# One first load for gains, two x tiles and the first weights, and four gate/up tiles held in single PSUM places

## The chip, the cores and the metric

The kernel runs on one core of one Trainium2 chip. A core has a matrix engine (TensorE, PE in the profile, its weight loads PEld), VectorE (DVE), ScalarE (ACT), GpSimd (POOL) and SyncE (SP, which only starts transfers here). Matmuls write to PSUM; DVE and ACT read it from there; all other data lies in SBUF, and transfers from HBM run on 16 DMA engines. The metric is the device time of one execution in microseconds, as the median of several.

## What is computed

Two layers of a decoder trunk on 256 tokens of width 1024, in float32. A layer is: half a gated feed-forward step, a mixing step (four retention heads and eight latent attention heads side by side), and another half feed-forward step. Cut to what matters for the change:

```python
def rms_norm(x, g):
    y = x * lax.rsqrt(jnp.mean(x * x, axis=-1, keepdims=True) + EPS)
    return y * g

def swiglu_ffn(h, w_gate, w_up, w_down):
    return (jax.nn.silu(h @ w_gate) * (h @ w_up)) @ w_down

for l in range(DEPTH):                     # DEPTH = 2, D_FF = 2816
    x = x + 0.5 * swiglu_ffn(rms_norm(x, ffn1_norm[l]), ffn1_w_gate[l], ffn1_w_up[l], ffn1_w_down[l])
    h = rms_norm(x, mix_norm[l])
    ...                                    # retention and attention, with rotary tables cos/sin of the positions
    x = x + jnp.concatenate([y_ret, y_mla], axis=-1) @ w_o[l]
    x = x + 0.5 * swiglu_ffn(rms_norm(x, ffn2_norm[l]), ffn2_w_gate[l], ffn2_w_up[l], ffn2_w_down[l])
```

## The kernel before

x lies transposed in SBUF, as eight tiles (d or k = 0 to 7) of 128 features by 256 tokens. Each float32 number is split into a high and a low part (`split`, L111 to L118): ACT writes the high part, DVE subtracts it from the original and writes the low part. A product of the two is then three terms: high weight by high x, low weight by high x, high weight by low x. One "block" multiplies one 128 by 128 weight block with one x tile. In the usual form it is two matmuls: the high weights stream both parts of x (512 columns), the low weights only the high part (256 columns). High by low lands in other PSUM columns than the rest and is added on eviction.

Weights come as units of 128 by 1024 numbers (512 KB), in the order of their use. `emit_unit` (L131) issues a unit's load on SP's queue into one of four raw buffers and splits it into one of seven pairs of high and low buffers; `get(i, ahead)` (L154) emits units up to `i + ahead`. Two units make one gate/up tile f (128 of the 2816 hidden features, gate and up): the first unit holds k = 0 to 3, the second k = 4 to 7. Units 0 to 3 come in two pieces each; between their pieces SP issues the gains (`gn`) and x in four loads of two tiles.

The norm is applied late. The matmuls run on x times the gain, and the factor 1/rms of each token is multiplied in when a gate/up tile is evicted. `prep` (L191) splits an x tile, `prep_sq` (L196) squares it and adds it up; for the first norm both run on POOL, for all others the square is on ACT and the sum on DVE. `rstd_of` (L227) adds over the partitions with two small matmuls (`ss`), `rstd_rows` takes the power -1/2 on POOL and puts it on a diagonal (`dg`), `rstd_bc` spreads it over the partitions with one matmul (`rb`) and an ACT copy (`rbc`).

`ffn` (L294) runs 22 gate/up tiles and then the down projection. `gu_mm` does a tile's matmuls; a tile's PSUM place has two banks, `ps2` holds two such places in turn. `gu_sum` (L321) copies one half of the sums by ACT and adds the other half by DVE, `gu_evict` (L331) multiplies with `rbc`, takes silu on ACT, multiplies gate by up and splits the result. For the very first feed-forward step (`first`) the tiles 0 to 2 go block by block (`block`), the squares' sum is taken after six k of tile 1 and the spread after three k of tile 2.

The order of the instructions on each engine is set at compile time by a scheduler that takes the program order as priority and fills gaps with later work; `issue_after` and hand-made dependencies without a semaphore tie it down in places. So the load of the constants (`cst`, masks, decays and rotary frequencies) and of the positions, and the rotary tables that `rope_tables` computes from them on DVE with one sine on ACT, come after the first feed-forward step in the program, but run inside it.

## Time and profile before

| | us |
|---|---|
| median of 3 runs | 932.96 (932.96 to 933.67) |
| profiled execution | 933.92 |
| its span, first to last instruction | 932.1 |
| PE busy in the span | 918.2 (99%) |
| PEld busy | 827.6 (89%) |
| DVE busy | 724.4 (78%) |
| ACT busy | 566.7 (61%) |
| POOL busy | 40.0 (4%) |

The busy share of PE contains waits inside pipelined matmuls, so it is an upper bound. A duration is that of one recorded instruction; back-to-back instructions of an engine overlap a little at their ends. "x8" after an instruction means that eight records are merged into one line. The name behind "<-" in brackets is what released an engine after it had been idle.

### The profile page before, as it was taken

To read this page: it belongs to the slowest core of one execution; us is meant where nothing else is said; L and a number is where in the kernel's file an instruction comes from. 1 tells how busy PE (TensorE), PEld (TensorE's weight loads), DVE (VectorE), ACT (ScalarE), POOL (GpSimd) and SP (SyncE) were. 2 spreads that over 40 slices of the span, in tenths; PEclk is the share of its full clock that TensorE was granted. 3 is DMA by queue.
4 is the path that set the end of the run, shared out by engine and by line. 5 is a ranking of instruction groups with operands and counts; after the bars stand their busy time and mean duration, and the time that the engine had idled before them with its cause. 6 is when DMAs were issued, how large, how long until landed. Compare 5 with 4: busy or idle time off the path is not lost.

```text
span 932.1 us, 14689 instructions
## 1 busy us (share of the span) xinstructions
PE 918.2 (99%) x5518; PEld 827.6 (89%) x5518; DVE 724.4 (78%) x1185; ACT 566.7 (61%) x945; POOL 40.0 (4%) x50
## 2 busy tenths in 40 slices
PE   7999999999999999999999999999999999999998
PEld 5988999998788999999999999999978899999998
DVE  6998886668869888886678888776697798888751
ACT  5665665466966666654556566554868575666540
POOL 6001000011100000000000000000000000000000
PEclk9999999999999999999999999999999999999999
DMA  6866666653534756666656566655545356656660
GB/s 233 279 215 195 212 215 214 184 176 112 178 114 134 233 199 202 203 195 213 202 182 203 193 210 191 217 186 181 174 136 158 105 168 213 209 191 208 204 195 23
DMA packets 49750, 173.79 MB, mean 186 GB/s; under 512 B 5648, under 2 KB 6800, under 8 KB 49680
## 3 DMA queue, kind: packets, MB, share of 16 engines
q1 hardware_dynamic: 49680, 172.87, 57.7%
q8 instruction: 43, 0.70, 0.3%
q14 instruction: 27, 0.22, 0.1%
HBM read 171.80 MB, written 1.05 MB: 185 GB/s over the span
## 4 chain that ended last, share of the span: by engine, by line
PE 85%; DVE 6%; DMA 2%; ACT 2%; POOL 2%; issue 1%; SPq 0%; POOLq 0%; ACTq 0%
PE gu L267 28%; PE dn L267 16%; PE gu L272 14%; PE dn L272 8%; PE wo L267 2%; DVE wlo L115 2%; DMA raw<-w 2%; ACT whi L114 1%; PE wo L272 1%; PE rk L473 1%; PE rv L474 1%; POOL acc L206 1%; PE rq L473 1%; PE qtr L642 1%; PE rk L474 1%
## 5 line engine op out<-in xcount | busy, mean ns | idle before, releaser
L115 DVE TENSOR_TENSOR wlo<-raw,whi 128x1024 fp32r<-128x1024 f32 (+2 forms) x316 | 375.6, 1211 | 63.0 <-ACT whi L114 62.7
L114 ACT ACTIVATE whi<-raw 128x1024 fp32r<-128x1024 f32 (+2 forms) x316 | 326.4, 1041 | 142.3 <-PE dn L267 86.8
L267 PE MATMUL gu<-xhl,whi 128*128 128x512 f32 x1360 | 311.3, 380 | 0.5 <-DVE gt L328 0.2
L267 PEld LDWEIGHTS gu<-xhl,whi 128*128 128x128 f32 x1360 | 249.9, 189 | 34.1 <-DVE gt L328 2.9
L272 PEld LDWEIGHTS gu<-xhl,wlo 128*128 128x128 f32 x1360 | 165.7, 192 | 4.8
L272 PE MATMUL gu<-xhl,wlo 128*128 128x256 f32 x1360 | 166.7, 275 | 0.0
L267 PE MATMUL dn<-h,whi 128*128 128x512 f32 x682 | 159.5, 379 | 0.0
L267 PEld LDWEIGHTS dn<-h,whi 128*128 128x128 f32 x682 | 123.7, 190 | 14.5
L114 ACT ACTIVATE h<-gh 128x256 fp32r<-128x256 f32 x88 | 36.6, 416 | 132.5 <-DVE gh L339 132.5
L272 PEld LDWEIGHTS dn<-h,wlo 128*128 128x128 f32 x682 | 87.0, 191 | 3.8
L272 PE MATMUL dn<-h,wlo 128*128 128x256 f32 x682 | 87.4, 275 | 0.0
L328 DVE TENSOR_TENSOR gt<-gu,ga 128x512 f32<-128x512 f32 x88 | 60.8, 690 | 20.6 <-ACT ga L326 19.8
L326 ACT ACTIVATE ga<-gu 128x512 f32<-128x512 f32 x88 | 52.2, 593 | 22.9 <-PE gu L256 7.9
L115 DVE TENSOR_TENSOR h<-gh,h 128x256 fp32r<-128x256 f32 x88 | 37.4, 425 | 35.7 <-ACT h L114 35.7
L335 DVE TENSOR_TENSOR gt<-gt,rbc 128x512 f32<-128x512 f32 x88 | 60.8, 691 | 2.9
L337 ACT ACTIVATE gs<-gt 128x256 f32<-128x256 f32 x88 | 35.6, 405 | 5.4 <-DVE gt L335 5.3
L339 DVE TENSOR_TENSOR gh<-gs,gt 128x256 f32<-128x256 f32 x88 | 36.9, 419 | 0.3 <-ACT gs L337 0.3
L291 DVE SCALAR_TENSOR_TENSOR x<-dn,x 128x256 f32<-128x256 f32 x31 | 12.7, 421 | 29.6 <-PE dn L267 29.6
L118 DVE SCALAR_TENSOR_TENSOR xhl<-x,gn,xhl 128x256 fp32r<-128x256 f32 x48 | 25.0, 532 | 1.0 <-ACT xhl L117 0.8
L117 ACT ACTIVATE whi<-raw,gn 128x256 fp32r<-128x256 f32 (+2 forms) x38 | 20.5, 579 | 8.1 <-PE ckq L475 4.5
L118 DVE SCALAR_TENSOR_TENSOR wlo<-raw,gn,whi 128x256 fp32r<-128x256 f32 (+2 forms) x38 | 20.8, 577 | 5.5 <-ACT whi L117 5.4
L117 ACT ACTIVATE xhl<-x,gn 128x256 fp32r<-128x256 f32 x48 | 23.4, 496 | 1.6 <-DMA x<-xT 1.0
(234 smaller groups left out, 936.5 us busy)
## 6 DMA issues: line engine op xcount, KB each, us to landing
raw<-w SPq DMA_DIRECT2D x310, 512.0 KB, 4.1
raw<-w SPq DMA_DIRECT2D x8, 416.0 KB, 3.3
raw<-w SPq DMA_DIRECT2D x8, 256.0 KB, 5.7
raw<-w SPq DMA_DIRECT2D x4, 384.0 KB, 3.1
x<-xT SPq DMA_DIRECT2D x4, 256.0 KB, 5.9
out_dram<-x SPq DMA_DIRECT2D x8, 128.0 KB, 2.2
cst<-cst SPq DMA_DIRECT2D x1, 1015.0 KB, 8.1
gn<-gains SPq DMA_DIRECT2D x1, 97.0 KB, 2.8
```

The source lines that it names most:

```text
L114: act(out=h, in_=x, func=AF.Copy)
L115: tt(out=lo, in0=x, in1=h.bitcast(F32), op=ALU.subtract)
L117: act(out=h, in_=x, func=AF.Copy, scale=gain)
L118: stt(out=lo, in0=x, scalar=gain, in1=h.bitcast(F32), op0=ALU.mult, op1=ALU.subtract)
L267: mm(out=ps, lhsT=hi, rhs=both(xhl), start=first, stop=last)
L272: mm(out=ps[:, :S], lhsT=lo, rhs=halves(xhl[:, 0]), start=False, stop=False)
L326: act(out=mem4(a), in_=mix4(ps[:, :, :S]), func=AF.Copy)
L328: tt(out=mem4(t), in0=mix4(ps[:, :, S:]), in1=mem4(a), op=ALU.add)
L335: tt(out=t, in0=t, in1=st.rbc.unsqueeze(1).broadcast_to([P, 2, S]), op=ALU.mult)
L337: act(out=s, in_=t[:, 0], func=AF.Silu)
L339: tt(out=hf, in0=s, in1=t[:, 1], op=ALU.mult)
L473: mm(out=o, lhsT=xh, rhs=wh, start=(k == 0), stop=False)
```

## The change

The gains, the first two x tiles and the first 128 by 256 weights become one DRAM array, loaded by one transfer of 128 rows of 962 numbers (481 KB). The order of the first loads is then: unit 2 (first half of tile f1), the rest of unit 0, x tiles 2 to 5, unit 1, unit 3, x tiles 6 and 7. Their splits follow a list written out by hand, and `program_order` keeps the order of the program on every engine inside its block.

The tiles f0 and f1 are multiplied side by side (`FIRST_ORDER`), then f2 and f3. Each block of these four tiles is three matmuls of 256 columns (`block3`) that add up in one PSUM place of one bank, so that two tiles share what one took. The squares are taken by ACT (`prep_sq_all`, three instructions) and added by DVE (three) after units 4 and 5 have been split. The sum over the partitions comes after seven k of f2, the spread after three k of f3; `gu_scale` evicts such a tile in one DVE instruction with the norm multiplied in, and so the four tiles stay in PSUM until the norm is there. Nothing of the norm is left on POOL but the power and the identity.

The rotary tables and their loads move from behind the first feed-forward step to behind its tile 14; the loads are tied behind the last weight load issued by then.

```diff
+FIRST_ORDER = [(0, 0), (1, 0), (1, 1), (0, 1)] + [(f, k) for k in range(2, KD) for f in range(2)]
...
+    @contextmanager
+    def program_order():
+        cur = nc.cur_bb
+        n = len(cur.bb.instructions)
+        yield
+        assert nc.cur_bb is cur
+        last = {}
+        for i in cur.bb.instructions[n:]:
+            if i.engine in last:
+                tc.add_manual_dep(i, last[i.engine].name,
+                                  mybir.DependencyInfo(mybir.DependencyClass.NoSync, mybir.DependencyReason.DATA),
+                                  reason="program_order")
+            last[i.engine] = i
...
+        skip = 2 * P if i == 0 else 0
+        last_load[0] = nc.sync.dma_start(out=raw[:, skip:n], in_=src[:, skip:])
         segs = gains or [(c, step, None) for c in range(0, n, step)]
-        for c, w, g in segs:
-            split(hi[:, c:c + w], lo[:, c:c + w], raw[:, c:c + w], g)
-        emitted.append((hi, lo))
+        if i == 0:
+            segs = [(0, skip, None), (skip, 2 * P, None), (4 * P, 4 * P, None)]
+        emitted[i] = (hi, lo)
+        return [lambda c=c, w=w, g=g: split(hi[:, c:c + w], lo[:, c:c + w], w00 if c < skip else raw[:, c:c + w], g)
+                for c, w, g in segs]
...
+    def prep_sq_all(st):
+        h = KD * S // 2
+        sq = [hp.tile([P, h], F32, tag=f"h{8 + i}", name=f"sqw{i}") for i in range(2)]
+        act(out=sq[0], in_=xt[:, :h], func=AF.Square)
+        act(out=sq[1][:, :2 * S], in_=x01, func=AF.Square)
+        act(out=sq[1][:, 2 * S:], in_=xt[:, h:], func=AF.Square)
+        tt(out=sq[0], in0=sq[0], in1=sq[1], op=ALU.add)
+        tt(out=sq[0][:, :2 * S], in0=sq[0][:, :2 * S], in1=sq[0][:, 2 * S:], op=ALU.add)
+        st.acc = tp.tile([P, S], F32, tag="acc", name="acc")
+        tt(out=st.acc, in0=sq[0][:, :S], in1=sq[0][:, S:2 * S], op=ALU.add)
...
+    def block3(o, hi, lo, xhl, first, last):
+        mm(out=o, lhsT=hi, rhs=halves(xhl[:, 0]), start=first, stop=False)
+        mm(out=o, lhsT=lo, rhs=halves(xhl[:, 0]), start=False, stop=False)
+        return mm(out=o, lhsT=hi, rhs=halves(xhl[:, 1]), start=False, stop=last)
...
+            if first and f < 4:
+                if f not in pgu:
+                    pgu[f // 2 * 2] = pgu[f // 2 * 2 + 1] = ps2(f"gu{f}")
+                ps = pgu[f][:, f % 2]
+                for k in ks:
+                    hi, lo = get(gu[2 * f + k // 4], 0)
+                    for j in range(2):
+                        c = slice((k % 4 * 2 + j) * P, (k % 4 * 2 + j + 1) * P)
+                        m = block3(ps[:, j * S:(j + 1) * S], hi[:, c], lo[:, c], st.xhl[k], k == 0 and j == 0, k == KD - 1 and j == 1)
+                return m
...
+            if first and f < 4:
+                rb4 = as_ts(st.rbc).unsqueeze(1).broadcast_to([P, 2, 2, P])
+                tt(out=mem4(t), in0=mix4(ps[:, f % 2].rearrange("p (j c) -> p j c", j=2)), in1=rb4, op=ALU.mult)
...
         if first:
-            m = gu_mm(1, range(6))
-            with tc.issue_after(m.ins):
+            with program_order():
+                for f, k in FIRST_ORDER:
+                    gu_mm(f, (k,))
+                get(gu[4], 0)
+                get(gu[5], 0)
+                prep_sq_all(st)
+                get(gu[6], 0)
+                get(gu[7], 0)
+                gu_mm(2, range(7))
                 rstd_of(st)
-            rstd_rows(st)
-            gu_mm(1, range(6, KD))
-            gu_sum(0)
-            m = gu_mm(2, range(3))
-            with tc.issue_after(m.ins):
+                rstd_rows(st)
+                get(gu[8], 0)
+                gu_mm(2, (7,))
+                gu_mm(3, range(3))
                 rstd_bc(st)
+                gu_scale(0)
+                gu_scale(1)
             gu_evict(0)
             gu_evict(1)
-            gu_mm(2, range(3, KD))
+            gu_mm(3, range(3, KD))
             gu_evict(2)
+            gu_evict(3)
...
+            if first and f == 14:
+                first()
...
-    get(0, 1)
-    for d in range(KD):
-        prep(d, st, gn[:, 0, G_F1 + d:G_F1 + d + 1])
-    get(3, 0)
-    for d in range(KD):
-        prep_sq(d, st, True)
+    order[:4] = [2, 0, 1, 3]
+    nc.sync.dma_start(out=head_t, in_=first_d)
+    pcs = {}
+    pcs[2] = load_unit(2)
+    pcs[0] = load_unit(0)
+    nc.sync.dma_start(out=xt[:, :4 * S], in_=xT_d[:, :4 * S])
+    pcs[1] = load_unit(1)
+    pcs[3] = load_unit(3)
+    nc.sync.dma_start(out=xt[:, 4 * S:], in_=xT_d[:, 4 * S:])
+    gp = lambda d: gn[:, 0, G_F1 + d:G_F1 + d + 1]
+    with program_order():
+        for i, d in ((0, 0), (2, 1), (0, None), (0, 2), (2, 3), (1, 4), (3, 5), (1, 6), (3, 7)):
+            pcs[i].pop(0)()
+            if d is not None:
+                prep(d, st, gp(d))
...
-            nc.sync.dma_start(out=cst, in_=cst_d)
-            nc.sync.dma_start(out=posi, in_=pos_d)
-            cs = rope_tables()
+            def tables():
+                with tc.issue_after(last_load[0].ins):
+                    nc.sync.dma_start(out=cst, in_=cst_d)
+                    nc.sync.dma_start(out=posi, in_=pos_d)
+                cs_.append(rope_tables())
+            cs_ = []
+            ffn(st, *e["f1"], n1, col(G_MIX), tables)
```

## Rows read from the trace of the kernel before

**Rows 1.** Busy time by stretch: start:end, length, each engine's busy time (records), clock, DMA.

```profile
core 0: us, PE busy (x) PEld busy (x) DVE busy (x) ACT busy (x) POOL busy (x), PEclk, DMA share, GB/s
6.78:22.36 15.58, 12.00 (x56) 8.53 (x56) 13.72 (x16) 8.84 (x16) 13.85 (x15) 1.00 0.74 265
...
48.00:83.00 35.00, 34.52 (x206) 29.84 (x205) 32.21 (x61) 21.16 (x35) 3.15 (x8) 1.00 0.64 196
83.00:131.00 48.00, 48.00 (x294) 44.03 (x293) 42.72 (x59) 30.46 (x49) 0.00 (x0) 1.00 0.64 214
131.00:932.00 801.00, 794.11 (x4792) 717.93 (x4790) 611.21 (x1016) 486.74 (x817) 20.32 (x17) 1.00 0.56 180
```

**Rows 2.** Timeline, PE's opening: start, duration, engine, line, instruction, count, what it waited for.

```profile
6.78 0.48 PE L252 MATMUL gu<-xhl,whi 128*128 128x512 f32 x1 [1.79 <-DVE xhl L118]
...
15.86 0.38 PE L252 MATMUL gu<-xhl,whi 128*128 128x512 f32 x1
...
20.29 0.38 PE L256 MATMUL gu<-xhl,whi 128*128 128x512 f32 x1
...
22.36 0.61 PE L231 MATMUL ss<-ones,acc 128*128 128x1 f32 x4 [1.69 <-POOL acc L206]
...
22.83 0.36 PE L255 MATMUL gu<-xhl,wlo 128*128 128x256 f32 x1
...
29.89 1.89 PE L267 MATMUL gu<-xhl,whi 128*128 128x512 f32 x8
```

**Rows 3.** Timeline, PE: the low-weight matmuls of tiles f3, f6, f12 and f13.

```profile
31.62 1.95 PE L272 MATMUL gu<-xhl,wlo 128*128 128x256 f32 x16
...
47.34 1.95 PE L272 MATMUL gu<-xhl,wlo 128*128 128x256 f32 x16
...
80.87 1.95 PE L272 MATMUL gu<-xhl,wlo 128*128 128x256 f32 x16
...
86.11 1.95 PE L272 MATMUL gu<-xhl,wlo 128*128 128x256 f32 x16
```

**Rows 4.** Timeline: first load's issue, first ACT splits, each released by a landing.

```profile
0.74 0.39 SPq L141 DMA_DIRECT2D raw<-w  x1
...
3.64 0.63 ACT L114 ACTIVATE whi<-raw 128x512 fp32r<-128x512 f32 x1 [1.41 <-DMA raw<-w]
...
5.28 0.91 ACT L117 ACTIVATE xhl<-x,gn 128x256 fp32r<-128x256 f32 x2 [1.00 <-DMA x<-xT]
...
7.68 0.63 ACT L114 ACTIVATE whi<-raw 128x512 fp32r<-128x512 f32 x1 [1.50 <-DMA raw<-w]
```

**Rows 5.** DMA, 0 to 12 us: rate in 40 slices of 0.3 us.

```profile
GB/s 0 0 0 0 0 41 130 300 292 310 224 325 219 164 212 178 198 198 198 164 123 137 225 321 355 341 335 376 396 382 410 403 403 403 403 396 376 423 382 396
```

**Rows 6.** DVE splits, min/median/max ns: weights to 14 us, x to 18, x later.

```profile
L115 DVE TENSOR_TENSOR wlo<-raw,whi x4: 679/693/1097, 4.3 to 12.4; 128x512 fp32r<-128x512 f32 x4
...
L118 DVE SCALAR_TENSOR_TENSOR xhl<-x,gn,xhl x8: 473/870/945, 5.8 to 14.2; 128x256 fp32r<-128x256 f32 x8
...
L118 DVE SCALAR_TENSOR_TENSOR xhl<-x,gn,xhl x16: 475/480/485, 149.3 to 301.0; 128x256 fp32r<-128x256 f32 x16
```

**Rows 7.** Timeline, PE at the end: first matmul of the first and last of 22 three-matmul blocks.

```profile
921.08 0.27 PE L399 MATMUL dn<-h,whi 128*128 128x256 f32 x1
...
928.11 0.28 PE L399 MATMUL dn<-h,whi 128*128 128x256 f32 x1
```

**Rows 8.** Timeline, the norm's chain: power on POOL, spread row on ACT.

```profile
23.25 0.71 POOL L216 TENSOR_TENSOR rstd<-ms,mhalf 128x2 f32<-128x2 f32 x1 [0.94 <-DVE ms L233]
...
26.82 0.38 ACT L247 ACTIVATE rbc<-rb 128x256 f32<-128x256 f32 x1
```

**Rows 9.** The constants' load (KB, us to landing), and a wait in 48 to 83 us.

```profile
cst<-cst SPq DMA_DIRECT2D x1, 1015.0 KB, 8.1
...
PEld gu L267 <- DVE gt L328: 2.9, 6, 0.6
```

**Rows 10.** Costliest groups of the page: the weight loads of the high parts.

```profile
L267 PEld LDWEIGHTS gu<-xhl,whi 128*128 128x128 f32 x1360 | 249.9, 189 | 34.1 <-DVE gt L328 2.9
```

More of the change, by code (lines that the diff above doesn't have):

```diff
@@ L1 @@
 import math
-from contextlib import ExitStack
+from contextlib import ExitStack, contextmanager
 import numpy as np
@@ L121, in body, with load_unit @@
     units = []
-    emitted = []
+    emitted = {}
+    order = []
     off = [0]
+    last_load = [None]
     def add_unit(ncols, pieces=1, gains=None):
         units.append((off[0], ncols, pieces, gains))
+        order.append(len(units) - 1)
         off[0] += ncols
         return len(units) - 1
-    def emit_unit():
-        o, n, pieces, gains = units[len(emitted)]
-        i = len(emitted)
+    def load_unit(i):
+        o, n, pieces, gains = units[i]
         assert n == WIDTHS[i]
@@ L138, in emit_unit @@
         step = n // pieces
-        dstep = step if i < 4 else n
-        for c in range(0, n, dstep):
-            nc.sync.dma_start(out=raw[:, c:c + dstep], in_=src[:, c:c + dstep])
-            if i == 0 and c == 0:
-                nc.sync.dma_start(out=gn, in_=gn_d)
-            if i < 2:
-                xs = slice(UW * i + c, UW * i + c + dstep)
-                nc.sync.dma_start(out=xt[:, xs], in_=xT_d[:, xs])
-        segs = gains or [(c, step, None) for c in range(0, n, step)]
-        for c, w, g in segs:
-            split(hi[:, c:c + w], lo[:, c:c + w], raw[:, c:c + w], g)
-        emitted.append((hi, lo))
+        skip = 2 * P if i == 0 else 0
+        last_load[0] = nc.sync.dma_start(out=raw[:, skip:n], in_=src[:, skip:])
+        segs = gains or [(c, step, None) for c in range(0, n, step)]
+        if i == 0:
[3 more added lines that the diff above has]
+                for c, w, g in segs]
     def get(i, ahead=2):
         while len(emitted) <= min(i + ahead, len(units) - 1):
-            emit_unit()
+            for piece in load_unit(order[len(emitted)]):
+                piece()
         return emitted[i]
-    xt = xp.tile([P, KD * S], F32, tag="x", name="x")
-    x = [xt[:, d * S:(d + 1) * S] for d in range(KD)]
-    gn = const.tile([P, L, GR], F32, name="gn")
+    head_t = const.tile([P, L * GR + 2 * S + 2 * P], F32, name="first")
+    gn = head_t[:, :L * GR].rearrange("p (l c) -> p l c", l=L)
+    x01 = head_t[:, L * GR:L * GR + 2 * S]
+    w00 = head_t[:, L * GR + 2 * S:]
+    xt = xp.tile([P, (KD - 2) * S], F32, tag="x", name="x")
+    x = [x01[:, d * S:(d + 1) * S] for d in range(2)] + [xt[:, d * S:(d + 1) * S] for d in range(KD - 2)]
     cst = const.tile([P, CW], F32, name="cst")
@@ L194, in prep, with prep_sq @@
         st.xhl.append(xhl)
[L196 removed]
+    def prep_sq(d, st):
         sq = tp.tile([P, S], F32, tag="sq", name="sq", bufs=3)
[L198 to L201 removed]
+        act(out=sq, in_=x[d], func=AF.Square)
         if d == 0:
@@ L247, in rstd_bc @@
         act(out=st.rbc, in_=pb[:, :S], func=AF.Copy)
-    def block(ps, hi, lo, xhl, k, last):
-        if k == 0:
-            mm(out=ps, lhsT=hi, rhs=both(xhl), start=True, stop=False)
-            mm(out=ps[:, :S], lhsT=lo, rhs=halves(xhl[:, 0]), start=False, stop=False)
-        else:
-            mm(out=ps[:, :S], lhsT=lo, rhs=halves(xhl[:, 0]), start=False, stop=False)
-            return mm(out=ps, lhsT=hi, rhs=both(xhl), start=False, stop=last)
+    def block3(o, hi, lo, xhl, first, last):
+        mm(out=o, lhsT=hi, rhs=halves(xhl[:, 0]), start=first, stop=False)
+        mm(out=o, lhsT=lo, rhs=halves(xhl[:, 0]), start=False, stop=False)
+        return mm(out=o, lhsT=hi, rhs=halves(xhl[:, 1]), start=False, stop=last)
     turn = [0]
@@ L301, in gu_mm @@
             ps = pgu[f]
-            if first and f < 3:
-                for k in ks:
-                    hi, lo = get(gu[2 * f + k // 4])
-                    for j in range(2):
-                        c = slice((k % 4 * 2 + j) * P, (k % 4 * 2 + j + 1) * P)
-                        m = block(ps[:, j], hi[:, c], lo[:, c], st.xhl[k], k, k == KD - 1)
-                return m
             for u in range(2):
@@ L367, in ffn @@
             gu_evict(1)
-        for f in range(3 if first else 2, NF):
+        for f in range(4 if first else 2, NF):
             gu_mm(f)
             gu_evict(f)
+            if first and f == 14:
+                first()
         pss = {}
```

48 lines of the change are left out of this document (24 added, 24 removed).

## The prediction

> **What bounds the kernel now.** I read the stages first: busy time by stretch of the span [rows 1]. From 83 us to the end TensorE (PE) has almost no idle time (48.00 of 48.00 us, then 794.11 of 801.00), so what follows the first feed-forward's opening is a rigid tail: what the opening saves moves the end by as much. In 6.78 to 22.36 us PE is busy for only 12.00 of 15.58 us, while VectorE (DVE) has 13.72 and GpSimd (POOL) 13.85. So I read PE in order of time next [rows 2]. Its first real matmul starts at 6.78 us and waited for the low half of x. Tile f0 (16 blocks, one for each of 8 k and of gate and up) lasts until 15.86. After 20.29 it waits for the sum of squares, whose two matmuls start at 22.36; f3 starts at 29.89. Then the los of one tile after the other [rows 3]: 31.62 to 47.34 us are three tiles of 5.24 us, 0.33 per block, with no stall. So f4 starts at 29.89 + 5.24 = 35.13. From 47.34 to 80.87 six tiles take 33.53 us instead of 31.44: 2.1 us are lost there, and tile 86.11 - 80.87 = 5.24 is normal again.
>
> PE's work up to f4 is 64 blocks x 0.33 = 21.1 us and twice 0.47 (22.83 - 22.36, [rows 2]; the broadcast of the norm taken at the same) = 22.0 us. It starts f4 at 35.13, so 13.1 us are lost: 6.78 before the first matmul, 15.86 - 6.78 - 5.3 = 3.8 in f0, the rest (2.5) in f1 and f2, mostly the wait for the squares.
>
> **The change part by part.** *First load.* Before, weights of 256 KB land at 3.64 us, and x lands at 5.28, by when 609 KB (two pieces and 97 KB of gains) have been asked for [rows 4]. One load of 481 KB lies between: 3.64 + 225/353 x 1.64 = 4.7 us. The first weight piece is half of the 0.63 us form, some 0.4 us of ScalarE (ACT), then half of the 0.91 us for two x tiles [rows 4]: the high halves are there at 5.5 us, first matmul 5.6, 1.2 us sooner. The trace shows 2.9 us from the issue of a 256 KB piece at 0.74 us to the split that it released at 3.64 [rows 4]. The Trainium skill, "DMA: Bandwidth & Descriptors", section "Anatomy of one DMA — SWDGE (gpsimd) path", fits about 2.0 us plus bytes over 436 GB/s (for another issuing path), an estimate of 2.6 us for 256 KB and 3.1 for 481 KB; by it the first load is there at 3.9 us and the forecast below would be 925.2 instead of 926.0. The measured piece is already 0.3 us over that fit, so I stay with the rows.
>
> *The loads behind it* are the unknown. In the 0.3 us slices of [rows 5] the transfers run at about 300 GB/s at first, fall to 120 to 220 between 4 and 6.6 us, and reach some 400 (0.66 us per 256 KB) from 8 us on; the next weight piece lands only at 7.6 [rows 4]. The new order is 512 KB (f1), 384 (rest of f0), 512 (x tiles 2 to 5), 512, 512, 256 KB. Fast end, no dip, 0.66 us per 256 KB from 4.7: landings at 6.0, 7.0, 8.3, 9.6, 10.9, 11.6. Slow end, the dip as before, 865 KB at 7.6 and then 0.66 per 256 KB: 7.9, 8.9, 10.2, 11.6, 12.9, 13.6. The dip stands where many small pieces are queued; larger ones may or may not meet it. I take a point a little nearer the fast end.
>
> *Splits without POOL.* The 16 squares and sums leave POOL. While POOL runs, an x split on DVE takes 0.87 us (median), later 0.48; a weight piece takes up to 1.10 against 0.69 [rows 6]. In the new order each k costs DVE one piece and one x, 0.69 + 0.48 = 1.17 us, ACT 0.63 + 0.46 = 1.09, and PE four blocks. So PE sets the pace as soon as the loads are there.
>
> *Four tiles in single places.* A block is three 256-column matmuls with three weight loads instead of 512 + 256 columns with two: the columns are the same. The end of the kernel already does this: from 921.08 to 928.11 are 21 blocks, 0.335 us each [rows 7]. So 64 blocks cost 21.4 instead of 21.1 us: +0.3. The Trainium skill, "TensorE: Matmul & The Clock Gate", Part 3, "The mechanism", says a weight load overlaps matmuls in flight only when the row group differs, which a full 128-row load can't offer; with the P/1.2 ns of its section on LDWEIGHTS, 107 ns for 128 columns, an estimate, the 64 extra loads would cost 6.8 us and the forecast would be 932.8. The trace disagrees: in [rows 7] the third load hides.
>
> *f0 and f1 side by side.* By hand, from these prices: fast end, x and weights for k = 0 to 2 of both tiles are done on PE at 10.7 us; these 12 blocks need 4.0 us from 5.6, so 1.1 us are lost; after that 20 blocks without a wait. Slow end: 12.8 us, 3.2 lost. f0 and f1 end at 17.4 or 19.5 us.
>
> *The norm's wait* moves behind f2's seventh k. ACT must first split units 4 and 5 (their loads wait for a raw buffer, free at about 10 us), then square; DVE splits both and adds three times. By my count ACT has the last x tile at 13.9 us (fast end) and needs 4.3 more for the two units and the squares (eight times 512 columns, 0.63 us each less the overlap, [rows 4]), DVE then 2.3 for sums of 1024, 512 and 256 columns (0.69 us for 512, [rows 6]): the sum is there at about 20.5 us, PE comes for it at 17.4 + 14 x 0.335 = 22.1: covered by 1.6 us. Before, PE stood 1.7 us for the last of POOL's sums [rows 2]. Then the rsqrt on POOL (0.71 us) and the diagonal on DVE, behind the splits of units 6 and 7, are done at 24.4; PE has two blocks of f2 and six of f3 until 25.3: covered by 0.9 us. The row of norms on ACT (0.38 us) [rows 8] and the two scales on DVE end at 27.7, while PE is in f3 until about 29: covered by 1.2 us. If this cover is gone, f4 waits for its PSUM place by what is over, and behind the scales on DVE stand the split of unit 9 and all evictions. Each of the four tiles also saves ACT's copy and one of DVE's four passes.
>
> f4 starts at 5.6 + lost 1.1 (3.2) + 21.4 + 0.9 = 29.0 (fast) or 31.1 (slow); I take 29.7, so 35.13 - 29.7 = 5.4 us gained.
>
> *The tables.* Their load of 1015 KB takes 8.1 us to land [rows 9], competed with the weight loads, and their small DVE steps ran in these six tiles, where DVE is busy for 32.21 of 35.00 us [rows 1] and PE waited six times for DVE to free a PSUM place [rows 9]: the 2.1 us of [rows 3]. Moved behind tile 14 they meet a DVE that is 42.72 of 48.00 us busy [rows 1] and has had eleven tiles to get ahead. They cost between nothing and the same 2.1; I take 0.4, so 1.7 us are gained.
>
> *Order made anew.* The scheduler lays out the rest again; its length can move a few tenths either way (6.9 us of idle PE in the tail, [rows 1]). I count nothing.
>
> Sum on the profiled span: 932.1 - 5.4 - 1.7 = 925.0. That execution took 933.92 us, 1.8 more than its span and 0.96 more than the median of 932.96, so on the median 932.96 - 7.1 = 925.9, say 926.0 us.
>
> **Rivals.** *Dip and tables stay.* The loads come at the slow end and the tables cost 2.1 again: gain 35.13 - 31.1 = 4.0, 929.0 us. For it: [rows 5] show the dip in the same microseconds, and DVE stays the second busiest. Against it: larger pieces, more slack.
>
> *The tables hold DVE (slower).* DVE runs in order. If its first table step stands in its queue before the 1015 KB have landed, DVE stands for up to 8.1 us [rows 9], and then the steps cost their 2.1: 10.2 us, where no eviction is ahead to cover it; the head still gives 5.4 and the old 2.1: 935.7 us. It decides against the change once DVE stands for more than about 7 us. Against it: before, the steps came well after the landing, and a tile's eviction in steady state has about 4 us of room (5.24 less the copy and the sum).
>
> *The extra weight loads show.* At the 189 ns that one load is recorded with [rows 10], 64 x 0.19 = 12.1 us on top: 938.1. Against it speak the 0.335 us of [rows 7]. The rule of the Trainium skill cited above stands behind it, with its smaller price.
>
> *Nothing comes through.* The new order of the mixing stage or the late evictions after f3 (four tiles at once on DVE) give back what the head gains: 933. The tail's 6.9 us of idle PE is small, so this needs new stalls.
>
> **How the numbers follow.** My forecast (926.0, reaching 924.2 to 927.6) 0.61; dip and tables stay (929.0) 0.24; nothing comes through 0.07; tables hold DVE 0.05; weight loads show 0.02; 0.01 beyond. The low end is the fast start, 6.1 + 2.1 = 8.2 us, with half a microsecond of luck in the order: 924.2. The high end takes in the second case with half a microsecond against it: 929.5. About 0.2% (1.9 us) is what a measurement of this kernel tells from no change. Faster by more: the first two cases and a little of the rest, 0.86; within: 0.07; slower: 0.07.
>
> **What would show it.** In the changed profile: first matmul at about 5.6 us; f0 and f1 done between 17 and 19.5 us; no wait of PE for the sum of squares, for the diagonal or for the scales; f4 at 29 to 31 us; POOL nearly idle in 5 to 22 us and x splits at 0.48 us; blocks at 0.335 us; tiles 5 to 13 at 5.24 us each; the tables' DVE steps after 75 us with less than 1 us of stall; from 131 us of before on, the same order of lengths. The granted clock is 1.00 in every stretch of [rows 1]; I expect no other. Wrong it would be if PE stands at f4 for the scales, or DVE for the tables.

## The result, and the profile after

| | before | after |
|---|---|---|
| median of 4 runs, us | 932.96 (932.68 to 933.67) | 926.43 (926.20 to 926.99) |
| profiled execution | 933.92 | 926.99 |
| its span | 932.1 | 925.1 |
| f4 starts at | 35.13 | 29.10 |
| f21's lows begin, to the end | 804.07 | 803.66 |

The ratio over all executions is 0.9924, with a 95% interval of 0.9913 to 0.9936; the medians alone give 0.9930. The changed kernel is 6.5 us, 0.7%, faster. The forecast was 926.0 us.

The stages first. The columns are start:end, length, each engine's busy time with its records, granted clock, DMA share, GB/s.

```profile
core 0: us, PE busy (x) PEld busy (x) DVE busy (x) ACT busy (x) POOL busy (x), PEclk, DMA share, GB/s
5.08:17.50 12.42, 12.01 (x99) 11.27 (x98) 10.68 (x19) 10.89 (x20) 0.00 (x0) 1.00 0.92 334
17.50:29.10 11.60, 11.60 (x105) 11.55 (x104) 10.16 (x15) 7.40 (x9) 0.71 (x1) 1.00 0.76 249
48.00:83.00 35.00, 34.90 (x212) 31.69 (x212) 30.51 (x51) 21.42 (x34) 0.00 (x0) 1.00 0.72 242
83.00:121.44 38.44, 38.19 (x230) 34.36 (x229) 35.95 (x59) 22.69 (x37) 4.92 (x8) 1.00 0.62 195
121.44:925.00 803.56, 797.06 (x4813) 720.74 (x4811) 613.94 (x1021) 489.80 (x822) 20.33 (x17) 1.00 0.57 181
```

These answer to [rows 1]. In the opening POOL has gone from 13.85 us busy to the 0.71 us of the power, DVE from 13.72 us in 15.58 to 10.68 in 12.42, and PE has 12.01 us in 12.42. From 17.50 to 29.10 us PE has no idle time at all. The last two stretches before f21 leave PE idle for 0.10 and 0.25 us; a busy PE also contains waits inside its pipeline, so the tiles' starts say more.

The timeline, cut to the steps of the prediction: start, duration, engine, line, instruction, count, and in brackets what it waited for. L281 to L283 are a block's three matmuls, L294 and L299 those of the usual tiles.

```profile
0.74 0.38 SPq L840 DMA_DIRECT2D first<-first  x1
...
4.22 0.42 ACT L131 ACTIVATE whi<-first 128x256 fp32r<-128x256 f32 x1 [1.99 <-DMA first<-first]
5.08 0.38 PE L281 MATMUL gu<-xhl,whi 128*128 128x256 f32 x1
...
17.50 0.28 PE L281 MATMUL gu<-xhl,whi 128*128 128x256 f32 x1
...
19.82 0.42 DVE L237 TENSOR_TENSOR acc<-sqw 128x256 f32<-128x256 f32 x1
22.19 0.50 PE L261 MATMUL ss<-ones,acc 128*128 128x1 f32 x4
22.73 0.16 DVE L263 TENSOR_SCALAR ms<-ss 128x2 f32<-128x2 f32 x1 [0.21 <-PE ss L261]
22.97 0.71 POOL L246 TENSOR_TENSOR rstd<-ms,mhalf 128x2 f32<-128x2 f32 x1 [18.36 <-DVE ms L263]
23.72 0.48 DVE L271 TENSOR_SCALAR dg<-ident,rstd 128x128 f32<-128x128 f32 x2 [0.83 <-POOL rstd L246]
24.12 3.49 DVE L132 TENSOR_TENSOR wlo<-raw,whi 128x1024 fp32r<-128x1024 f32 x3
25.32 0.60 PE L275 MATMUL rb<-dg,ones 128*128 128x256 f32 x2
25.95 0.39 ACT L277 ACTIVATE rbc<-rb 128x256 f32<-128x256 f32 x1
27.52 1.28 DVE L358 TENSOR_TENSOR gt<-gu,rbc 128x512 f32<-128x512 f32 x2
29.10 1.89 PE L294 MATMUL gu<-xhl,whi 128*128 128x512 f32 x8
30.83 1.95 PE L299 MATMUL gu<-xhl,wlo 128*128 128x256 f32 x16
...
41.31 1.95 PE L299 MATMUL gu<-xhl,wlo 128*128 128x256 f32 x16
...
44.36 0.69 DVE L362 TENSOR_TENSOR gt<-gu,ga 128x512 f32<-128x512 f32 x1
...
46.93 1.95 PE L299 MATMUL gu<-xhl,wlo 128*128 128x256 f32 x16
...
76.29 0.17 DVE L462 CAST pf<-posi 128x2 f32<-128x2 int32 x1 [2.06 <-DMA posi<-pos]
78.37 1.95 PE L299 MATMUL gu<-xhl,wlo 128*128 128x256 f32 x16
...
95.24 1.95 PE L299 MATMUL gu<-xhl,wlo 128*128 128x256 f32 x16
...
121.44 1.95 PE L299 MATMUL gu<-xhl,wlo 128*128 128x256 f32 x16
```

Against [rows 2] the head reads thus: first matmul at 5.08 instead of 6.78 us, f2 begun at 17.50, and no bracket behind the sum of squares (`ss`), the spread (`rb`) or f4. f4 starts 35.13 - 29.10 = 6.03 us sooner. The low-weight matmuls (lows) of one tile after the other answer to [rows 3]: 46.93 - 41.31 = 5.62 where a free tile takes 5.24, so f7 loses 0.38; from 78.37 (f13) to 95.24 (f16) three tiles take 16.87 instead of 15.72, a loss of 1.15, while DVE does the steps of the tables (76.3 to 95.9 us). Together 1.53, against 2.09 before: only 0.56 gained in this execution. From f21 on 0.41 is gained. 6.03 + 0.56 + 0.41 = 7.00 = 932.1 - 925.1.

Two changes show in rows of their own. The transfers, 0 to 12 us in slices of 0.3 us:

```profile
GB/s 0 0 0 0 0 77 77 77 205 410 359 398 435 396 410 423 410 379 410 352 277 386 382 423 355 423 396 437 369 410 410 410 423 403 417 423 396 410 369 232
```

The dip of [rows 5] (120 to 220 GB/s between 4 and 6.6 us) is gone; some 400 GB/s flow from 2.7 us on. And the splits on DVE from 4 to 16 us, by shape: out<-in, shapes, count | busy us, mean ns | idle before.

```profile
L132 DVE TENSOR_TENSOR wlo<-raw,whi 128x512 fp32r<-128x512 f32 x7 | 4.8, 688 | 0.8 <-ACT whi L131 0.6
L135 DVE SCALAR_TENSOR_TENSOR xhl<-x,first,xhl 128x256 fp32r<-128x256 f32 x6 | 2.9, 478 | 0.2 <-ACT xhl L134 0.2
```

An x split takes 478 ns; with POOL beside it the median was 870 [rows 6].

### The profile page after: what moved, and what is told of

Its sections match the earlier page's. It is cut to its first block, busy times and chain, and to the rows that moved or that the text cites. A ratio compares the mean times of both kernels' runs of the same rounds, so it can differ in the third digit from the quotient of the medians.

```text
span 925.1 us, 14786 instructions
## 1 busy us (share of the span) xinstructions
PE 916.6 (99%) x5582; PEld 830.5 (90%) x5582; DVE 718.4 (78%) x1185; ACT 567.1 (61%) x945; POOL 27.0 (3%) x35
## 3 DMA queue, kind: packets, MB, share of 16 engines
HBM read 171.80 MB, written 1.05 MB: 187 GB/s over the span
## 4 chain that ended last, share of the span: by engine, by line
PE 85%; DVE 8%; DMA 2%; ACT 2%; issue 1%; POOL 1%; SPq 0%; POOLq 0%; DVEq 0%; ACTq 0%
PE gu L294 26%; PE dn L294 16%; PE gu L299 14%; PE dn L299 8%; DVE wlo L132 3%; PE wo L294 2%; DMA raw<-w 2%; ACT whi L131 1%; PE wo L299 1%; PE qtr L687 1%; DMA posi<-pos 1%; PE rk L518 1%; PE rv L519 1%; PE rk L519 1%; PE rq L518 1%
## 5 line engine op out<-in xcount | busy, mean ns | idle before, releaser
L294 PE MATMUL gu<-xhl,whi 128*128 128x512 f32 x1344 | 307.1, 380 | 0.5
L294 PEld LDWEIGHTS gu<-xhl,whi 128*128 128x128 f32 x1344 | 246.9, 189 | 33.1 <-DVE gt L362 2.1
L299 PEld LDWEIGHTS gu<-xhl,wlo 128*128 128x128 f32 x1344 | 163.7, 192 | 4.7
L299 PE MATMUL gu<-xhl,wlo 128*128 128x256 f32 x1344 | 164.7, 275 | 0.0
L294 PE MATMUL dn<-h,whi 128*128 128x512 f32 x682 | 159.4, 379 | 0.0
L294 PEld LDWEIGHTS dn<-h,whi 128*128 128x128 f32 x682 | 123.7, 190 | 14.5
L299 PEld LDWEIGHTS dn<-h,wlo 128*128 128x128 f32 x682 | 87.0, 191 | 3.7
L299 PE MATMUL dn<-h,wlo 128*128 128x256 f32 x682 | 87.4, 275 | 0.0
L362 DVE TENSOR_TENSOR gt<-gu,ga 128x512 f32<-128x512 f32 x84 | 58.0, 690 | 19.8 <-ACT ga L361 19.1
L363 DVE TENSOR_TENSOR gt<-gt,rbc 128x512 f32<-128x512 f32 x84 | 58.0, 691 | 2.8
L318 DVE SCALAR_TENSOR_TENSOR x<-dn,x 128x256 f32<-128x256 f32 x23 | 9.7, 422 | 29.6 <-PE dn L294 29.6
L134 ACT ACTIVATE whi<-raw,first 128x256 fp32r<-128x256 f32 (+2 forms) x38 | 20.4, 578 | 8.2 <-PE ckq L520 4.5
L135 DVE SCALAR_TENSOR_TENSOR wlo<-raw,first,whi 128x256 fp32r<-128x256 f32 (+2 forms) x38 | 20.8, 577 | 5.5 <-ACT whi L134 5.4
L134 ACT ACTIVATE xhl<-x,first 128x256 fp32r<-128x256 f32 x36 | 17.8, 494 | 1.0 <-DVE x L316 0.6
L281 PE MATMUL gu<-xhl,whi 128*128 128x256 f32 x64 | 18.2, 284 | 0.0
```

Source lines behind the costliest of these rows:

```text
L134: act(out=h, in_=x, func=AF.Copy, scale=gain)
L135: stt(out=lo, in0=x, scalar=gain, in1=h.bitcast(F32), op0=ALU.mult, op1=ALU.subtract)
L294: mm(out=ps, lhsT=hi, rhs=both(xhl), start=first, stop=last)
L299: mm(out=ps[:, :S], lhsT=lo, rhs=halves(xhl[:, 0]), start=False, stop=False)
L362: tt(out=mem4(t), in0=mix4(ps[:, :, S:]), in1=mem4(a), op=ALU.add)
L363: tt(out=t, in0=t, in1=st.rbc.unsqueeze(1).broadcast_to([P, 2, S]), op=ALU.mult)
```

## The experiments

Theory A is the prediction's: the head gives its microseconds because POOL is quiet, the loads come evenly, f0 and f1 run side by side and four tiles fit into two places; the tables cost what they cost because their steps meet a DVE without slack. Theory B is for each run the rival written beside it. The first five runs each undo one part of the head, and f4's start is where to look; the others move the tables. Unless said otherwise an edit is to the changed kernel. The kernel before, run beside them, took 933.85 to 934.15 us (medians). Each of the first five is a single execution, and all losses by tile are those of single traces. Three expectations give 16.5 us for f2 in the changed kernel; its trace has 17.50.

**Squares back on POOL.** The three wide squares and sums become sixteen POOL instructions, in the place where the change has them.

```diff
-                prep_sq_all(st)
+                for d in range(KD):
+                    sq = tp.tile([P, S], F32, tag="sq", name="sq", bufs=3)
+                    nc.gpsimd.tensor_tensor(out=sq, in0=x[d], in1=x[d], op=ALU.mult)
...
+                        nc.gpsimd.tensor_tensor(out=acc, in0=st.acc, in1=sq, op=ALU.add)
```

> The changed kernel, but the sixteen squares and sums of the first norm on GpSimd again, one x tile at a time. In the changed kernel f4 starts at 29.1 us and the span is 925.1. Theory A (GpSimd beside VectorE stretches VectorE's splits): splits go back from 0.48 and 0.69 us towards 0.79 and 0.97 (the means of before), 1.76 per k instead of 1.17, over the 1.34 us that PE needs; f0 and f1 take some 3 us more, f4 starts at 32 to 33, span 928 to 929. Theory B (only PE's wait for the sum counts): GpSimd starts one us sooner than before and is done at 21 to 22 us, when PE asks for the sum at 22.2; f4 stays within 0.5 us of 29.1, span 925 to 925.6.

Measured: 931.24 us, span 929.3; f2 at 20.22, f4 at 32.51, 3.4 later than in the changed kernel. PE did not wait for the squares. The same groups of DVE, 4 to 16 us:

```profile
L132 DVE TENSOR_TENSOR wlo<-raw,whi 128x512 fp32r<-128x512 f32 x6 | 6.8, 1126 | 0.2 <-ACT whi L131 0.2
L135 DVE SCALAR_TENSOR_TENSOR xhl<-x,first,xhl 128x256 fp32r<-128x256 f32 x4 | 3.3, 832 | 0.0
```

1126 against 688 ns, 832 against 478, and DVE has next to no idle time before them (0.2 us): here POOL costs nothing by a wait for its sums and 3.4 us by the lengthened splits next to it. Theory A holds.

**One tile after the other.** f0 with all its k, then f1; loads and splits as they are.

```diff
-FIRST_ORDER = [(0, 0), (1, 0), (1, 1), (0, 1)] + [(f, k) for k in range(2, KD) for f in range(2)]
+FIRST_ORDER = [(f, k) for f in range(2) for k in range(KD)]
```

> The changed kernel, but on PE f0 with its eight k first and then f1; loads and splits in the same order. Theory A (two tiles side by side give PE 1.34 us of work per k, which covers the 1.17 us that VectorE needs for it): f0 alone has 0.67 us per k, so it ends with the last split at about 15 us, and f1 takes 5.4 us after that: f2 starts at about 20.3 instead of 16.5, f4 at about 32.9, span some 3.8 longer, 928.9. Theory B (the early start is what counts, PE catches up later): f4 within 1 us of 29.1, span under 926.

Measured: 932.04 us, span 930.3; f2 at 20.91 and f4 at 32.51, again 3.4 later; f0 ends with the last splits, at about 15.5 us, and f1 follows whole. The span grew by 5.2, since the tiles f7 (0.89) and the tables (2.08) lost more too. Theory A holds for f4, but with something beside it. The windows of 8 to 12 us (columns as above):

```profile
8.00:9.00 1.00, 0.92 (x4) 0.74 (x4) 0.90 (x2) 0.65 (x2) 0.00 (x0) 0.57 1.00 406
9.00:11.00 2.00, 2.00 (x12) 2.00 (x11) 1.79 (x4) 1.98 (x5) 0.00 (x0) 0.50 1.04 404
11.00:12.00 1.00, 1.00 (x8) 1.00 (x8) 0.91 (x3) 0.80 (x2) 0.00 (x0) 0.72 0.91 352
```

PE had waited 1.46 us before 7.81 for a split; then its granted clock was 0.57, 0.50 and 0.72, the lower of its two levels (1.2 GHz) in the middle stretch. The trace shows that this cost next to nothing at f0's end: from 13 us on PE stands for each split again (at 13.00, 14.00 and 15.00 a matmul starts 0.05 us after a split of x on DVE has ended, at 12.95, 13.95 and 14.95), and the last split ends only 0.3 us later than in the changed kernel (14.66). The 3.4 us are thus the order's.

**Own places for the first four tiles.** The usual two-matmul blocks, a place of its own for each tile, f0 and f1 summed without the norm as soon as they are done, and scaled later.

```diff
-                    pgu[f // 2 * 2] = pgu[f // 2 * 2 + 1] = ps2(f"gu{f}")
-                ps = pgu[f][:, f % 2]
+                    pgu[f] = ps2(f"gu{f}")
+                ps = pgu[f]
...
-                        m = block3(ps[:, j * S:(j + 1) * S], hi[:, c], lo[:, c], st.xhl[k], k == 0 and j == 0, k == KD - 1 and j == 1)
+                        m = block(ps[:, j], hi[:, c], lo[:, c], st.xhl[k], k, k == KD - 1)
...
+                gu_sum(0)
+                gu_sum(1)
                 prep_sq_all(st)
```

> The changed kernel, but the first four tiles use the usual blocks (512 and 256 columns, two weight loads) and a whole PSUM place each; f0 and f1 are summed into SBUF unscaled by ScalarE and VectorE before f2 can start, and scaled later. Theory A (what holding four tiles in single places buys is that PE needn't wait for a place): 64 blocks are 0.5 us cheaper, but f2 waits for the sum of f0 until about 17.9 us instead of 16.5, and the norm's chain comes some 1.5 us later, so f4 starts at 30 to 31, span 926 to 927. Theory B (the place is no matter, the blocks are): f4 at 28.6, span 924.6.

Measured: 929.50 us, span 927.7; f2 at 18.07, f4 at 32.39 us. Theory A, and larger than I expected: I had counted a wait of f2 for a place, which came at 0.76 us, and missed the one of f4. Timeline of PE and waits from 5 to 36 us (engine line <- releaser: us in all, times, longest):

```profile
18.07 0.48 PE L282 MATMUL gu<-xhl,whi 128*128 128x512 f32 x1 [0.76 <-DVE gt L368]
...
32.39 1.97 PE L302 MATMUL gu<-xhl,whi 128*128 128x512 f32 x8 [2.33 <-DVE gt L368]
```

```profile
PEld gu L302 <- ACT ga L367: 2.6, 1, 2.6
PE gu L302 <- DVE gt L368: 2.3, 1, 2.3
```

This is what the prediction named for a gone cover, "f4 waits for its PSUM place", made real: the eviction of f2 by copy and sum comes too late (on DVE at 31.56, behind the scales and evictions of f0 and f1). With the sums where this edit puts them, ahead of the squares, holding tiles in single places is worth 3.3 us at f4. The same run speaks on the tables as well: DVE stood 1.52 us for the positions, and no tile lost anything to them.

**Half pieces.** The opening's weights and x tiles 2 to 5 are asked for in halves.

```diff
-        last_load[0] = nc.sync.dma_start(out=raw[:, skip:n], in_=src[:, skip:])
+        for c0, c1 in ([(skip, n // 2), (n // 2, n)] if i < 4 else [(skip, n)]):
+            last_load[0] = nc.sync.dma_start(out=raw[:, c0:c1], in_=src[:, c0:c1])
...
-    nc.sync.dma_start(out=xt[:, :4 * S], in_=xT_d[:, :4 * S])
+    for c in (0, 2 * S):
+        nc.sync.dma_start(out=xt[:, c:c + 2 * S], in_=xT_d[:, c:c + 2 * S])
```

> The changed kernel, but units 2, 0, 1, 3 and x tiles 2 to 5 in two loads each (rows of 2 KB, as before), in the same order, the first load as it is. In the changed kernel the transfers rise to 400 GB/s at 2.7 us and stay there; before, they fell to 120 to 220 GB/s between 4 and 6.6 us. Theory A (many small pieces in the queue make the dip): the dip is back, x tile 2 is there some 1.5 to 2 us later than at 8.3 us, f0 and f1 end at 18 to 19 us instead of 16.5, span 926.5 to 927.5. Theory B (the gains' own load of 776-byte rows made the dip): no dip, span 925 to 925.4.

Measured: 928.40 us, span 926.6. The rate from 0 to 12 us:

```profile
GB/s 0 0 0 0 0 64 115 115 218 359 372 387 243 191 253 335 376 335 277 307 386 382 389 410 403 396 341 335 341 382 396 430 410 369 410 410 369 430 417 410
```

A short dip is back (243, 191, 253), yet f2 starts at 17.48 and the squares are asked for at 22.17, both as before the edit. The 1.5 us came later: f4 waited 0.35 us and began at 29.59, f5 lost 0.66, f8 0.38, the tables 1.43. Neither theory holds as it was put: smaller pieces do bring a dip, but one of this length is covered. What of the later loss is the pieces' and what is a schedule that came out otherwise stays open.

**First load in three.** Weights, gains and x of the first load separately, in that order.

```diff
-    nc.sync.dma_start(out=head_t, in_=first_d)
+    for c0, c1 in ((L * GR + 2 * S, L * GR + 2 * S + 2 * P), (0, L * GR), (L * GR, L * GR + 2 * S)):
+        nc.sync.dma_start(out=head_t[:, c0:c1], in_=first_d[:, c0:c1])
```

> The changed kernel, but its first load comes as three (128 by 256 weights with 1 KB rows, the gains with 776-byte rows, two x tiles with 2 KB rows); all other loads as in the change. In the changed kernel the first split starts at 4.2 us and f4 at 29.1 us. Theory A (small rows at the start make the dip of the kernel before): the first weights are there earlier, at 3.2 to 3.6 us, but the transfers fall to 120 to 220 GB/s between 4 and 6.6 us, x tile 2 comes 1 to 2 us later than at 8.3 us, f2 starts at 18.5 to 19.5 instead of 17.5, f4 at 30 to 31. Theory B (the dip needs the many 2 KB pieces of the weights behind it too): no dip, f4 within 0.3 us of 29.1.

Measured: 928.44 us, span 926.6. The timeline of x's first split, the rate and one window:

```profile
5.60 0.51 ACT L134 ACTIVATE xhl<-first 128x256 fp32r<-128x256 f32 x1 [2.26 <-DMA first<-first]
```

```profile
GB/s 0 0 0 0 0 24 140 282 222 183 143 287 396 246 205 348 362 358 338 338 386 191 246 365 386 416 410 396 437 410 423 410 423 423 403 389 369 389 341 294
```

```profile
9.00:11.00 2.00, 2.00 (x11) 2.00 (x11) 1.69 (x4) 1.64 (x5) 0.00 (x0) 0.50 1.00 408
```

The first weights were there at 2.92 us, sooner, but x only at 5.60: the first matmul waits for the last of three, at 6.16, 1.1 us later than in the changed kernel. The last split of x ends 1.1 us later too (15.78 against 14.66). f4 starts at 31.51, 2.4 later. Here too the granted clock fell, to 0.50 in 9 to 11 us, and from 8.95 to 12.15 us 15 matmuls in a row start 0.21 us apart instead of 0.11, so about 1.3 of the 2.4 fall to the slow stretch (an estimate: 2.4 less the 1.1). The span grew by only 1.5, since f7 lost nothing here and the tables 0.42. Broadly theory A, with a part that it did not have: one load is worth 1.1 us by its landing, and whether it also keeps the clock up is not shown.

**Tables behind the feed-forward step, as in the kernel before, with the new head.**

```diff
-            def tables():
-                with tc.issue_after(last_load[0].ins):
...
-            ffn(st, *e["f1"], n1, col(G_MIX), tables)
+            ffn(st, *e["f1"], n1, col(G_MIX), lambda: None)
+            nc.sync.dma_start(out=cst, in_=cst_d)
+            nc.sync.dma_start(out=posi, in_=pos_d)
+            cs = rope_tables()
```

> The changed kernel, but the tables and their loads stand behind the first feed-forward step again, as in the kernel before, so that the scheduler starts the load among the early weight loads. In the changed kernel tiles f5 to f20 lose 1.5 us in all: 0.4 at f7 and 1.15 in three tiles in which the tables' steps run. Theory A (the move of the tables is worth the difference of the two losses): the tiles lose some 2.1 us as before, span 925.7, median 927.0. Theory B (the tables' loss before came from the head's backlog, which is shorter now): the loss stays at 1.5 or falls, span 924.5 to 925.1.

Measured: 928.66 us, ratio to the kernel before 0.9943 (0.9928 to 0.9958). Timeline of PE, the lows of f5 to f8:

```profile
36.14 1.95 PE L299 MATMUL gu<-xhl,wlo 128*128 128x256 f32 x16
41.93 1.95 PE L299 MATMUL gu<-xhl,wlo 128*128 128x256 f32 x16
48.48 1.95 PE L299 MATMUL gu<-xhl,wlo 128*128 128x256 f32 x16
53.76 1.95 PE L299 MATMUL gu<-xhl,wlo 128*128 128x256 f32 x16
```

f6 takes 5.79 and f7 6.55 us instead of 5.24; with four later tiles (0.20, 0.37, 0.29, 0.40) and 0.04 at f8 the loss is 3.16. So the move is worth 3.16 - 1.53 = 1.6 us in the new kernel, although the comparison with the old trace shows only 0.56. But the old place in the program is not the old place in time. The issue of the constants' load, here and, below it, in the kernel before:

```profile
10.55 0.43 SPq L862 DMA_DIRECT2D cst<-cst  x1
```

```profile
28.89 0.42 SPq L808 DMA_DIRECT2D cst<-cst  x1
```

With nothing to tie it, the scheduler issues the load 18 us sooner, among the first weights, and f6 and f7 lose 1.86 us before the first step of the tables runs at 54.99 (f7 0.27 before). From f8 on, where the steps run, the loss is 1.30 here (to f13) and 1.82 before (to f12), so the steps themselves did not become dearer. That the early load costs f6 and f7 is likely, since PE waits there for sums behind weight splits that come late; no run shows it alone. Of the two theories A is the nearer, since the loss neither stayed nor fell; that it rose, A did not say either.

**Early load.** Positions and constants are loaded behind tile 8, the steps stay behind tile 14 in the program.

```diff
-            if first and f == 14:
-                first()
+            if first and f in (8, 14):
+                first(f // 14)
```

> The changed kernel, but the positions and the constants are loaded behind tile 8's weights, positions first, and the tables stay behind tile 14. In the changed kernel VectorE's first table step stands 2.06 us for the positions, which were queued behind the 1015 KB. Theory A (this stand uses up the room that VectorE had gained, and so PE waits): no stand, the three slowed tiles lose under 0.3 us instead of 1.15, span 924.2, median 925.5. Theory B (the steps' own 6 us are too much for VectorE's room in any case): the loss stays at about 1.1 us, span 925.1.

Measured: 927.88 us, ratio 0.9935 (0.9921 to 0.9950). DVE no longer stands for the positions, but as soon as the data are early the scheduler pulls the steps forward: the first runs at 49.20 instead of 76.29 us. f7 loses 0.39 before that, as in the changed kernel, and f8 to f11, where the steps run, lose 0.50, 0.50, 0.29, 0.28 = 1.57 us. Theory A fails as tested: without any stand the steps cost at least as much. But they run in other tiles here, so this run alone does not part the stand from the place.

**The kernel before with the tables moved.** An edit to the kernel before: loads and steps behind tile 14, the steps in the buffers that they have in the change, nothing else.

```diff
+            if first and f == 14:
+                first()
...
-            nc.sync.dma_start(out=cst, in_=cst_d)
-            nc.sync.dma_start(out=posi, in_=pos_d)
-            cs = rope_tables()
+            ffn(st, *e["f1"], n1, col(G_MIX), tables)
```

> The kernel before with one part of the change alone: the tables behind tile 14, their loads tied behind the last weight load. Theory A (the parts add): the 2.1 us lost in f7 to f12 become 1 to 1.5 us in f13 to f16, span 931.0 to 931.5, median 932. Theory B (the weight loads that the constants no longer delay give more): over 1.5 us gained, span under 930.6.

Measured: 933.42 us beside 934.09, ratio 0.9990 (0.9981 to 0.9999). In its trace the tables cost 0.35 us in one tile instead of 2.09, so the tiles give 1.7, as the prediction said and more than theory A. The median moved by 0.7 only, as theory A had it, and the ten executions spread from 931.76 to 934.84, over more than either gain: neither theory is decided. The profiled execution itself (934.22) lost 2.1 us in its opening, where PE waited 2.50 us before its first real matmul at 7.44 and then ran at a lower clock:

```profile
7.00:9.00 2.00, 1.56 (x5) 1.38 (x6) 0.99 (x3) 0.84 (x2) 0.27 (x2) 0.61 1.00 336
9.00:11.00 2.00, 2.00 (x9) 1.62 (x9) 2.00 (x3) 2.00 (x6) 2.00 (x3) 0.54 1.05 405
...
21.00:23.00 2.00, 0.30 (x3) 0.19 (x2) 1.18 (x1) 0.00 (x0) 1.68 (x2) 1.00 0.69 211
23.00:25.00 2.00, 2.00 (x13) 1.83 (x13) 0.71 (x3) 0.00 (x0) 0.71 (x1) 0.87 0.75 223
25.00:35.00 10.00, 10.00 (x55) 9.04 (x54) 9.60 (x15) 8.42 (x13) 0.00 (x0) 0.85 0.67 223
```

**Tables in the down projection.** Loads behind tile 14, positions first; the steps 24 blocks into the down projection in the order of the program.

```diff
+            if first and b == 24:
+                first(1)
```

> The changed kernel, but the tables' steps come 24 blocks into the down projection, where VectorE has less to do; their loads are issued behind tile 14's weights as in the change. Theory A (in the down projection VectorE has room for them): no tile loses anything to the tables, only the 0.4 us at f7 stay, span 923.9 to 924.2, median 925.3. Theory B (the scheduler pulls the steps forward into the gate/up tiles as far as their loads allow): the loss of about 1.1 us stays, span 925.

Measured: 926.79 us, ratio 0.9921 (0.9905 to 0.9938). The place in the program did not hold: the scheduler filled gaps with them from 74.16 us on, where DVE stood 1.65 and then 1.42 us for data. The tables cost 0.78, f5 and f7 lost 0.41 and 0.68. Theory B, with a loss somewhat under its 1.1: nothing is gained over the changed kernel.

**Tied down.** The same, but the steps are tied behind the last weight split of tile 21.

```diff
+            if first and f == NF - 1:
+                with tc.issue_after(last_split[0].ins):
+                    first(1)
```

> The changed kernel, but the tables' steps are tied behind the last split of tile 21, so that they run in the down projection; the positions and the constants are loaded behind tile 14's weights, positions first. Theory A (the tables cost what they take from VectorE's room in the gate/up tiles; in the down projection there is enough): f13 to f21 lose nothing, the down projection neither, 1.1 us gained on the changed kernel run beside it. Theory B (the loss moves with the steps into the down projection): within 0.3 us of the changed kernel.

Measured: 926.09 us (925.68 to 926.60), ratio 0.9916 (0.9903 to 0.9930). Timeline of DVE and PE:

```profile
41.53 1.95 PE L301 MATMUL gu<-xhl,wlo 128*128 128x256 f32 x16
47.53 1.95 PE L301 MATMUL gu<-xhl,wlo 128*128 128x256 f32 x16
...
120.89 1.95 PE L301 MATMUL gu<-xhl,wlo 128*128 128x256 f32 x16
...
130.42 0.16 DVE L467 CAST pf<-posi 128x2 f32<-128x2 int32 x1
...
131.89 1.22 DVE L134 TENSOR_TENSOR wlo<-raw,whi 128x1024 fp32r<-128x1024 f32 x1
```

From 47.53 to 120.89 there are fourteen tiles of 5.24 us exactly, and from f21's lows to the end it takes 803.8 us, against 803.7 and 803.9 in the two traces of the changed kernel: here the tables cost nothing, as theory A says. f7 takes 6.00 us, though, 0.76 lost, and the 1.1 us that theory A wanted over the changed kernel beside it did not come (next run).

**The changed kernel again,** beside the last one and the load in three, as their common measure.

> The changed kernel itself, for comparison on the same chip as the tied tables. Both theories: ratio to the kernel before 0.992 to 0.994; f4 at 29.1 us; the clock granted throughout at its upper level, where the kernel before, whose PE waits for x from 5 to 6.8 us or longer, shows a mean of 0.996 to 0.998 in most executions.

Measured: 926.26 us (925.95 to 927.18), ratio 0.9920 (0.9907 to 0.9934). f4 at 28.88; f7 lost 0.20, the tables 0.38, though DVE stood 1.71 us. So the same kernel loses 0.38 or 1.15 us to its tables, by the execution, and differences of that size between single traces say little. Tying the tables down is 0.2 us better in the medians, which these intervals don't resolve.

## Why the prediction came out right, step by step

| step | predicted | measured |
|---|---|---|
| first load there, us | 4.7 | 4.22 |
| first matmul | 5.6 | 5.08 |
| lost in f0 and f1 | 1.1 (fast) to 3.2 | 1.7 |
| f2 starts | 17.4 (fast) to 19.5 | 17.50 |
| a three-matmul block | 0.335 | 0.33 |
| sum of squares: ready, asked for | 20.5, 22.1 | 20.24, 22.19 |
| cover of the diagonal | 0.9 | 1.1 |
| scales end; cover | 27.7; 1.2 | 28.80; 0.3 |
| f4 starts | 29.7 (29.0 to 31.1) | 29.10 |
| gain in the tiles to f21 | 1.7 | 0.56 |
| gain in the rest | 0 | 0.41 |
| sum on the span | 7.1 | 7.0 |

The time was met to 0.4 us in the median and the span to 0.1, but in the profiled execution by errors of opposite sign, and that is luck. The head gave 6.03 us instead of 5.4: the loads came at the fast end throughout, which I had taken only in part, and the first one half a microsecond sooner still. The tables gave 0.56 instead of 1.7: the term "I take 0.4" for what is left of their 2.1 us was 1.15 in this trace, and 0.38 at f7 was not in the sum at all. The 0.41 us of the rest were put at nothing. The second trace of the same kernel shows how loose the small terms are: there the head gave 35.13 - 28.88 = 6.25, the tiles 2.09 - 0.58 = 1.51 and the rest 0.14, together 7.9 on the span.

What f7 lacks is the sum of f5. It starts on DVE at 44.36, 1.0 us after ACT's copy of it is done, behind a unit split of 1.2 us begun at 43.23. The prediction wanted tiles 5 to 13 at 5.24 us each; for f7 that was wrong.

*First load.* Between the issue at 0.74 and the split at 4.22 us lie 3.5 us. The interpolation between rows of before had it at 4.7. The fit cited in the prediction from the Trainium skill, "DMA: Bandwidth & Descriptors", section "Anatomy of one DMA — SWDGE (gpsimd) path", would have it at 3.9 us, an estimate; the row lies between, nearer the fit. What a single load is worth is shown by the run in three: 1.1 us by its landing, and 2.4 at f4 with a stretch at the lower clock.

*Loads.* The case with the dip did not come. That piece size has a part in it is shown as far as halves brought some of it back; that the dip decided f4 is not, since the halves left f2 where it was.

*Splits without POOL.* Shown by the run with the squares on POOL, 3.4 us at f4. The prediction had priced the lengthening right (0.87 against 0.48 us) and worked it into the pace of f0 and f1.

*Blocks of three matmuls.* From 17.50 to 29.10 us are 32 blocks, `ss` and `rb`: (11.60 - 0.50 - 0.60) / 32 = 0.33 us a block. The rival that the weight loads show (0.19 us each) is out. The statement of the Trainium skill, "TensorE: Matmul & The Clock Gate", Part 3, "The mechanism", by which a third load of all rows could not hide, is out with it: the trace disagrees here as it did in [rows 7]. The same section, a paragraph earlier, and the page's Part 2, "Step-by-step: what each phase is for", let a load also run ahead into a background weight buffer; with that the trace agrees.

*Cover of the scales.* Thinner than said: DVE took three unit splits (3.49 us from 24.12) ahead of the two scales, so these ended 1.1 us late and only 0.3 us before PE came. Nothing was lost, but the run with own places shows what lies beyond: 2.3 us of waiting at f4.

*The tables hold DVE.* The rival came true in small: DVE stood 2.06 us for the positions, which landed 8.1 us after their issue. The prediction had asked for less than 1 us of stall and called itself wrong "if PE stands at f4 for the scales, or DVE for the tables"; on the tables it was wrong by that sign. The rival's own terms (steps 2.1, gains 5.4 and 2.1) put the stand that decides at 5.4 us, not at the 7 given there. The experiments part the stand's length from the loss. With a stand of 1.52 us no tile lost anything (own places) and with 1.71 the loss was 0.38 (the changed kernel again), but with 1.41 it was 1.17 (squares on POOL), with 1.43 also 1.43 (half pieces), with 2.06 1.15, with 2.31 2.08 (one tile after the other), and with none 1.57 in other tiles (early load). So the length of the stand does not set what is paid. What is shown is that the steps cost nothing in the down projection (tied down), where DVE still splits units between them but has no gate/up tiles to evict; why the same steps cost 0 to 2 us in the tiles stays open. DVE's backlog when they come is my guess and was not tried.

*The parts of the head don't add up.* Undone one by one they cost 3.4, 3.4, 3.3 and 2.4 us at f4, 12.5 together, where the whole head gained 6.03. Undone alone, each brings back a wait that the whole head had none of: DVE's longer splits, f1 behind the whole of f0, f4 behind the eviction of f2, the first matmul behind the last of three loads; the last figure also holds some 1.3 us of the lower clock.

## What to carry to other kernels

Where two engines work side by side, price what one does to the other's instructions, not only who waits for whom: moving sixteen small operations off GpSimd was worth 3.4 us though TensorE no longer waited for their result. An opening is worth packing (one load with all that the first matmul needs, tiles side by side as data arrive, sums held back in the fewest places), and its parts should be planned together: here four of them, left out one at a time, cost 2.4 to 3.4 us each, of a gain of 6. When a head gets shorter, look again at loads that only the scheduler places: with the tables in their old place of the program the tiles lost 2.1 us before and 3.2 with the new head, with the constants' load issued at 10.6 instead of 28.9 us.
